# Softmax weights turned by VectorE and DMA instead of TensorE, in a two-layer hybrid trunk on one core

## The chip, the cores and the metric

The kernel runs on one core of one Trainium2 chip, as one launch. The metric is the device time of the whole program in microseconds, lower being better. The engines are TensorE (PE, with its weight loads shown as PEld), VectorE (DVE), ScalarE (ACT), GpSimd (POOL) and SyncE (SP, which only issues DMAs here). Each works through its own queue strictly in order and waits for the others through semaphores.

## The reference

The input is 256 tokens of width 2048, in float32. Layer one is a gated DeltaNet mixer, layer two a chunked softmax attention with 16 heads of width 128; each adds its output to its input. The part that matters is layer two (condensed):

```python
proj = rms_norm(h, norm_w[1]) @ w_in                  # 2048 -> 4 * 2048: q, k, v, z
q, k = rms_norm(q, q_norm_w), rms_norm(k, k_norm_w)   # per head
s = einsum('bchd,bmhd->bhcm', q_n, k_n) * scale + bias
p = softmax(where(valid, s, -inf))                    # each frame: its own and earlier chunks
o = einsum('bhcm,bmhd->bchd', p, v_n)
h = h + (o * silu(z)) @ w_out
```

With 256 tokens every earlier chunk lies in the band, so the attention is causal by chunks of 64. A head's weights are 128 queries by 128 keys for the first half of the tokens and 128 by 256 for the second: 384 columns on 128 partitions.

## The kernel before

Activations are kept with features on partitions and tokens along the row. All projections run as split float32: each weight chunk (512 KB, 128 rows of 1024 floats in SBUF) is loaded by SP into `wt` (4 buffers), rounded by ACT into `whi` (L206) and the rest taken by DVE into `wlo` (L207), 3 buffers each. PE then does the matmuls of L255 on them. Chunks are fetched three ahead (`LOOK`). A cast of a new chunk waits until PE has finished with the chunk three before it; a load waits until DVE has finished with the one four before it.

Layer two's q, k and v are projected by blocks of 512 columns, four heads each, with tokens on partitions: k and q of group 0, then of groups 1, 2 and 3, then v of groups 0 to 3. A block is 8 chunks of 12 matmuls. All other work of a group is put behind those matmuls in small steps (a queue of generators, `bgq`, stepped between matmuls), and the scheduler that builds the program sets the final order on each engine:

- `qk_norm`: the square (ACT, L1051) into a buffer named `cv`, the sum (DVE, L1054), the reciprocal root (POOL, L1056 and L1058), the product (DVE, L1063) into another `cv`, the transposes (PE, L1073). There are two `cv` buffers.
- `attend`: for each head the scores (PE, L1092 and L1093), bias and maximum (DVE, L1101), exponentials with their sums (ACT, L1105), the division (DVE, L1111 and L1113). Then `turned`: three 128 by 128 transposes (PE, L1119) into PSUM and a copy (ACT, L1120) to the place that `weights_of` gives: heads 0 to 9 in `kT`, heads 10 to 15 in `dl`.
- `values`, after each v block: for each head two matmuls (L1149 and L1150) of the values with the turned weights, then the gate (DVE, ACT).

A float32 matmul of L1092, L1093, L1149 or L1150 is two instructions in the trace; a transpose is one.

Of the kernel before, what the change touches and what calls it, by code (L numbers as in the profile page):

```python
# [7 lines left out]
F32 = mybir.dt.float32  # L8
# [6 lines left out]
P = 128  # L15
D = 2048
# [22 lines left out]
def tile_hybrid_trunk(  # L39
# [11 lines left out]
    nc = tc.nc  # L51
    act, dve, pool, pe = nc.scalar, nc.vector, nc.gpsimd, nc.tensor
# [9 lines left out]
    def ps_small():  # L62
        return pss.tile([P, 512], F32, name="pss", tag="pss")

    def wk(tag, bufs=None):

        return work.tile([P, 4, T], F32, name=tag, tag=tag, bufs=bufs)

    def slot(tag, kb, dt=F32):

        return big.tile([P, kb * 256], dt, name=tag, tag=tag)
# [15 lines left out]
    ps = ps_small()  # L87
# [4 lines left out]
    ident = const.tile([P, P], F32, name="ident")  # L92
# [222 lines left out]
    def block(kind, xb, rate=1, pre=None):  # L315
        ps = acc(kind)
        for _ in range(CPH if kind == "half" else CPB):
            chunk(kind, ps, xb, rate, pre)
        return ps
# [10 lines left out]
    def pair(xb, rate=1, pre=None):  # L330

        evs = []
        for _ in range(2):
            joined(block("half", xb, rate, pre), evs)
        return evs
# [72 lines left out]
    rows = ctx.enter_context(tc.tile_pool(name="rows", bufs=1, space=bass.MemoryType.DRAM))  # L408
# [379 lines left out]
    def gated_tiles():  # L788
        gmem["b"] = slot("g", 32, F32R).rearrange("p (h a t) -> p h a t", h=H, a=2)
        gmem["h"], gmem["l"] = (gmem["b"][:, :, a, :] for a in range(2))  # L790
# [132 lines left out]
    for gi in range(4):  # L923
        if gi == 0:
            bgq.append(x_stats())
        ps = pair(xb, 2) if gi else block("features", xb, pre=x_split)
# [12 lines left out]
    for gi in range(4):  # L939
        ps = pair(xb, 2)  # L940
# [6 lines left out]
    hmem = {}  # L947
# [36 lines left out]
    bmem = {}  # L984
# [33 lines left out]
    def zb_small(gi, evs):  # L1018
        z = bmem["z"][:, 4 * gi:4 * gi + 4, :]
        scaled(z, evs, scales["h"][1])  # L1020

        bias, hs = bmem["bias"], slice(4 * gi, 4 * gi + 4)
        dve.tensor_copy(out=bias[0:1, 4 * gi, 0:1], in_=z[0:1, 0, 0:1])
        nc.gpsimd.dma_start(out=bias[:, hs, :], in_=relb[:, hs, :])
        pool.memset(bias[0:64, hs, 192:256], NEG)
        yield 1
        act.activation(out=z, in_=z, func=AF.Silu)
        yield 1
# [14 lines left out]
    for j in (1, 2, 3):  # L1043
        bgq.append(zb_small(j, pair(xb)))

    def qk_norm(ps, scale, dst):

        ssn = tiny.tile([P, 2, 4], F32, name="ssn", tag="so")
        rn = tiny.tile([P, 2, 4], F32, name="rn", tag="ro")
        sq = wk("cv").rearrange("p h t -> p (h t)")  # L1050
        act.activation(out=sq, in_=ps.rearrange("p t d -> p (t d)"), func=AF.Square)  # L1051
        yield 1
        yield 1
        dve.reduce_sum(out=ssn, in_=sq.rearrange("p (t h d) -> p t h d", t=2, d=P), axis=AX.X)  # L1054
        for t in range(2):
            pool.tensor_scalar(out=ssn[:, t, :], in0=ssn[:, t, :], scalar1=1.0 / P, scalar2=bmem["uh"][:, t:t + 1],  # L1056
                               op0=ALU.mult, op1=ALU.add)
        pool.tensor_tensor(out=rn, in0=ssn, in1=nhalf[:, :8].rearrange("p (t h) -> p t h", t=2), op=ALU.pow)  # L1058
        yield 1
        yield 1  # L1060
        n = wk("cv").rearrange("p h t -> p (h t)").rearrange("p (t d) -> p t d", t=2)
        for t in range(2):
            dve.tensor_tensor(out=n[:, t, :].rearrange("p (h d) -> p h d", d=P),  # L1063
                              in0=ps[:, t, :].rearrange("p (h d) -> p h d", d=P),
                              in1=rn[:, t, :].unsqueeze(2).broadcast_to([P, 4, P]), op=ALU.mult)
        yield 1
        yield 1
        for p in range(2):
            pt = ps_small()
            for i in range(2):  # L1070
                c = (2 * p + i) * P
                for t in range(2):
                    pe.transpose(pt[:, i * T + t * P:i * T + (t + 1) * P], n[:, t, c:c + P], ident)  # L1073
            d = dst[:, 2 * p:2 * p + 2, :].rearrange("p h t -> p (h t)")
            if scale is None:
                act.copy(out=d, in_=pt)
            else:
                act.activation(out=d, in_=pt, func=AF.Copy, scale=scale)
            yield 1

    def attend(gi, qn, kn):
        if gi == 0:
            gated_tiles()
            gmem["done"] = 0
            bmem["w"] = slot("kT", 16)
        st = {}

        def scores(i):
            h = 4 * gi + i
            bias = bmem["bias"]  # L1090
            ps = ps_small()
            pe.matmul(ps[:, 0:128], lhsT=qn[:, i, 0:128], rhs=kn[:, i, 0:128], start=True, stop=True)  # L1092
            pe.matmul(ps[:, 128:384], lhsT=qn[:, i, 128:256], rhs=kn[:, i, :], start=True, stop=True)  # L1093
            if i == 0:
                st["s"] = wk("raw", 1).rearrange("p h t -> p (h t)")
            s = st["s"][:, 384 * (i % 2):384 * (i % 2 + 1)]
            mx = tiny.tile([P, 2], F32, name="mx", tag="mx")
            sums = tiny.tile([P, 2], F32, name="sums", tag="sums")
            parts = ((0, 128, bias[:, h, 128:256]), (128, 384, bias[:, h, :]))
            for t, (a, b, bi) in enumerate(parts):  # L1100
                dve.tensor_tensor_reduce(out=s[:, a:b], in0=ps[:, a:b], in1=bi, scale=1.0, scalar=-3e38,  # L1101
                                         op0=ALU.add, op1=ALU.max, accum_out=mx[:, t:t + 1])
            dve.tensor_scalar(out=mx, in0=mx, scalar1=-1.0, scalar2=None, op0=ALU.mult)
            for t, (a, b, _) in enumerate(parts):
                act.activation(out=s[:, a:b], in_=s[:, a:b], func=AF.Exp, bias=mx[:, t:t + 1],  # L1105
                               accum_out=sums[:, t:t + 1])
            st[i] = (s, sums)

        def weights(i):
            s, sums = st[i]  # L1110
            dve.reciprocal(out=sums, in_=sums)  # L1111
            for t, (a, b) in enumerate(((0, 128), (128, 384))):
                dve.tensor_scalar(out=s[:, a:b], in0=s[:, a:b], scalar1=sums[:, t:t + 1], scalar2=None, op0=ALU.mult)  # L1113

        def turned(i):
            s, _ = st[i]
            ps = ps_small()
            for a in (0, 128, 256):
                pe.transpose(ps[:, a:a + P], s[:, a:a + P], ident)  # L1119
            act.copy(out=weights_of(4 * gi + i), in_=ps[:, :384])  # L1120

        stages = (scores, weights, turned)
        for n in range(4 + len(stages) - 1):
            for k in reversed(range(len(stages))):
                if 0 <= n - k < 4:
                    stages[k](n - k)
            yield 1

    def weights_of(h):

        if h < 10:
            return bmem["w"][:, 384 * h:384 * h + 384]
        c = 2 * D + 384 * (h - 10)
        return hmem["m"][:, c:c + 384]

    def vb_small(gi, ps):
        c = (8192, 10240, 9216, 11264)[gi]
# [6 lines left out]
    def values(gi):  # L1144
        v = bmem["v"]
        for h in range(4 * gi, 4 * gi + 4):
            pT, vs = weights_of(h), slice(h % 4 * P, (h % 4 + 1) * P)
            ps = ps_small()
            pe.matmul(ps[:, 0:256], lhsT=v[:, 0, vs], rhs=pT[:, 0:256], start=True, stop=False)  # L1149
            pe.matmul(ps[:, 128:256], lhsT=v[:, 1, vs], rhs=pT[:, 256:384], start=False, stop=True)  # L1150
            gt = work.tile([P, T], F32, name="gt", tag="gt")
            dve.tensor_tensor(out=gt, in0=ps[:, :T], in1=bmem["z"][:, h, :], op=ALU.mult)
            act.copy(out=gmem["h"][:, h, :], in_=gt)
            dve.tensor_tensor(out=gmem["l"][:, h, :], in0=gt, in1=gmem["h"][:, h, :].bitcast(F32), op=ALU.subtract)
            gmem["done"] = h + 1
            yield 1

    for gi in range(4):
        c = 1024 * (gi % 2)
# [10 lines left out]
    for gi in range(4):  # L1170
        bgq.append(vb_small(gi, block("tokens", xb)))
        bgq.append(values(gi))
# [28 lines left out]
    ps = [ps_small().rearrange("p (a t) -> p a t", a=2) for _ in range(2)]  # L1201
# [6 lines left out]
    for s in range(2):  # L1208
# [3 lines left out]
        for j, kt in enumerate(ks):  # L1212
            stop = kt == KT - 1
# [7 lines left out]
        for j, kt in enumerate(ks):  # L1221
            pe.matmul(ps[s][:, 0, :], lhsT=lo[:, j, fs], rhs=gmem["b"][:, kt, 0, :], start=False,
                      stop=kt == KT - 1, skip_group_check=True)
# [46 lines left out]
```

## Time and profile before

| | us |
|---|---|
| median of 3 runs | 997.7 |
| lowest and highest | 997.11, 998.75 |
| the profiled execution | 998.12 |
| its span in the trace | 996.4 |
| PE busy | 990.2 |
| DVE busy | 685.7 |
| ACT busy | 537.3 |
| POOL busy | 71.2 |

The profiled execution's own time is 1.7 us above the span of its instructions. A row of a group gives line, engine, operation, output and inputs, shape and count, then busy time and the mean of one in ns, then the engine's idle time before them and what ended it. A row of a timeline starts with the start in us from the span's start and the duration of the merged instructions. A row of DMA issues ends with the KB of one and the median us from issue to landing. The k, q and v blocks of layer two lie between about 630 and 910 us; the 48 transposes of L1119 lie between 677.9 and 837 us.

### The profile page before, as it was taken

To read this page: it belongs to the slowest core of one execution; us is meant where nothing else is said; L and a number is where in the kernel's file an instruction comes from. 1 tells how busy PE (TensorE), PEld (TensorE's weight loads), DVE (VectorE), ACT (ScalarE), POOL (GpSimd) and SP (SyncE) were. 2 spreads that over 40 slices of the span, in tenths; PEclk is the share of its full clock that TensorE was granted. 3 is DMA by queue.
4 is the path that set the end of the run, shared out by engine and by line. 5 is a ranking of instruction groups with operands and counts; after the bars stand their busy time and mean duration, and the time that the engine had idled before them with its cause. 6 is when DMAs were issued, how large, how long until landed. Compare 5 with 4: busy or idle time off the path is not lost.

```text
span 996.4 us, 15340 instructions
## 1 busy us (share of the span) xinstructions
PE 990.2 (99%) x5915; PEld 862.7 (87%) x5915; DVE 685.7 (69%) x1114; ACT 537.3 (54%) x769; POOL 71.2 (7%) x97
## 2 busy tenths in 40 slices
PE   9999999999999999999999999999999999999998
PEld 7988888888888898899888888888888888888887
DVE  7788787997999768665776555556565656555554
ACT  8455887655447556445654444446454545444442
POOL 1002100122000001100000000110101010000000
PEclk9999999999999999999999999999999999999999
DMA  9668775545666543447666676665656555555672
GB/s 291 190 169 237 211 209 162 156 148 169 190 192 172 139 135 106 142 142 242 214 190 199 205 213 210 188 190 151 187 152 186 158 181 148 171 177 172 212 221 83
DMA packets 138953, 179.67 MB, mean 180 GB/s; under 512 B 8048, under 2 KB 98560, under 8 KB 138880
## 3 DMA queue, kind: packets, MB, share of 16 engines
q1 hardware_dynamic: 136832, 172.12, 58.0%
q0 software_dynamic: 1760, 6.31, 1.8%
q8 instruction: 46, 0.75, 0.3%
q10 hardware_dynamic: 288, 0.26, 0.1%
q14 instruction: 27, 0.22, 0.1%
HBM read 176.56 MB, written 2.11 MB: 179 GB/s over the span
## 4 chain that ended last, share of the span: by engine, by line
PE 97%; ACT 1%; DMA 1%; issue 1%; DVE 0%; SPq 0%
PE psp L255 86%; PE pss L601 2%; PE pss L255 1%; PE pss L838 1%; PE pss L1073 1%; PE pss L1093 1%; PE pss L1149 1%; DMA g<-in_xT_dram 1%; PE pss L1119 1%; ACT whi L206 1%; PE pss L737 0%; PE pss L824 0%; PE pss L845 0%; PE pss L861 0%; PE pss L860 0%
## 5 line engine op out<-in xcount | busy, mean ns | idle before, releaser
L207 DVE TENSOR_TENSOR wlo<-wt,whi 128x1024 fp32r<-128x1024 f32 (+2 forms) x324 | 390.9, 1210 | 248.2 <-ACT whi L206 246.7
L206 ACT CAST whi<-wt 128x1024 fp32r<-128x1024 f32 (+2 forms) x324 | 336.6, 1040 | 371.4 <-PE psp L255 331.1
L255 PE MATMUL psp<-whi,xb 128*128 128x512 f32 x1024 | 320.3, 392 | 0.0
L255 PE MATMUL psp<-xb,whi 128*128 128x512 f32 (+1 forms) x1088 | 258.3, 381 | 0.5 <-ACT whi L206 0.3
L255 PEld LDWEIGHTS psp<-xb,whi 128*128 128x128 f32 x1088 | 196.0, 190 | 34.7 <-ACT whi L206 0.8
L255 PEld LDWEIGHTS psp<-whi,xb 128*128 128x128 f32 x1024 | 192.1, 188 | 38.8
L255 PE MATMUL psp<-wlo,xb 128*128 128x512 f32 x512 | 200.9, 392 | 0.0
L255 PE MATMUL psp<-xb,wlo 128*128 128x256 f32 x1024 | 147.5, 285 | 0.7 <-DVE wlo L207 0.6
L255 PEld LDWEIGHTS psp<-xb,wlo 128*128 128x128 f32 x1024 | 137.0, 191 | 7.0 <-DVE wlo L207 1.8
L255 PE MATMUL psp<-g,whi 128*128 128x512 f32 (+1 forms) x608 | 131.6, 347 | 0.2 <-DVE ev L326 0.2
L255 PEld LDWEIGHTS psp<-g,whi 128*128 128x128 f32 x608 | 104.4, 190 | 13.0 <-DVE ev L326 0.6
L255 PEld LDWEIGHTS psp<-wlo,xb 128*128 128x128 f32 x512 | 96.2, 188 | 19.3
L255 PE MATMUL psp<-g,wlo 128*128 128x256 f32 x480 | 82.3, 283 | 0.0
L255 PEld LDWEIGHTS psp<-g,wlo 128*128 128x128 f32 x480 | 69.8, 191 | 1.8
L518 DVE SCALAR_TENSOR_TENSOR cv<-raw,sm,cv 128x255 f32<-128x255 f32 (+2 forms) x144 | 64.0, 480 | 5.2 <-ACT cv L516 4.9
L516 ACT ACTIVATE cv<-raw,sm 128x256 f32<-128x256 f32 x48 | 22.2, 501 | 10.4 <-DVE raw L341 10.4
L326 DVE TENSOR_TENSOR ev<-psp,ev 128x512 f32<-128x512 f32 x37 | 25.3, 683 | 0.1
L325 ACT COPY ev<-psp 128x512 f32<-128x512 f32 x37 | 21.4, 579 | 2.5 <-DVE raw L341 2.5
L1056 POOL TENSOR_SCALAR ssn<-ssn,uh 128x4 f32<-128x4 f32 x16 | 9.2, 592 | 171.6 <-DVE ssn L1054 171.6
L605 DVE TENSOR_TENSOR dl<-pss,dl 128x512 f32<-128x512 f32 (+1 forms) x32 | 16.5, 551 | 1.6 <-PE pss L601 1.6
L873 POOL TENSOR_TENSOR ro<-so,nhalf 128x8 f32<-128x8 f32 x4 | 8.4, 2104 | 122.4 <-DVE so L871 122.4
L1063 DVE TENSOR_TENSOR cv<-psp,rn 128x512 f32<-128x512 f32 x16 | 10.3, 684 | 9.2 <-POOL rn L1058 9.2
(246 smaller groups left out, 734.1 us busy)
## 6 DMA issues: line engine op xcount, KB each, us to landing
wt<-in_b_w_in_dram SPq DMA_DIRECT2D x128, 512.0 KB, 3.7
wt<-in_a_w_in_dram SPq DMA_DIRECT2D x125, 512.0 KB, 4.1
wt<-in_a_w_out_dram SPq DMA_DIRECT2D x32, 512.0 KB, 3.9
wt<-in_b_w_out_dram SPq DMA_DIRECT2D x32, 512.0 KB, 3.5
tt<-line POOLq DMA_DIRECT2D x4, 512.0 KB, 9.1
dl<-in_xT_dram POOLq DMA_DIRECT2D x4, 512.0 KB, 5.9
dl<-in_relb_dram POOLq DMA_DIRECT2D x4, 512.0 KB, 5.0
g<-in_xT_dram SPq DMA_DIRECT2D x7, 256.0 KB, 6.6
```

The costliest lines, as they stand in the source:

```text
L206: cast = act.copy(out=hi[:, js, cs], in_=wt[:, js, cs])
L207: rest = dve.tensor_tensor(out=lo[:, js, cs], in0=wt[:, js, cs], in1=hi[:, js, cs].bitcast(F32), op=ALU.subtract)
L255: state["mm"] = pe.matmul(*args, **kw).ins
L325: act.copy(out=ev, in_=ps[:, :, 1, :])
L326: dve.tensor_tensor(out=ev, in0=ps[:, :, 0, :], in1=ev, op=ALU.add)
L516: act.activation(out=cv[:, i, :], in_=raw[:, i, :], func=AF.Copy, scale=conv_w(i0 + i, 3))
L518: dve.scalar_tensor_tensor(out=cv[:, i, s:], in0=raw[:, i, :T - s], scalar=conv_w(i0 + i, 3 - s), in1=cv[:, i, s:], op0=ALU.mult, op1=ALU.add)
L601: pe.matmul(dst, lhsT=kq[:, a, i, c:c + P], rhs=rhs, start=(n == 0), stop=(n == 2))
L605: dve.tensor_tensor(out=dl[:, h, :, c], in0=src.rearrange("p (k c) -> p k c", k=2), in1=dec[:, h, c].unsqueeze(1).broadcast_to([P, 2, n]), ...
L838: pe.matmul(ps[:, i * P:(i + 1) * P], lhsT=tt[:, 2 * (h0 + i) + t, :], rhs=vb[:, i, t, :], start=True, stop=True)
L1063: dve.tensor_tensor(out=n[:, t, :].rearrange("p (h d) -> p h d", d=P), in0=ps[:, t, :].rearrange("p (h d) -> p h d", d=P), in1=rn[:, t, :] ...
L1073: pe.transpose(pt[:, i * T + t * P:i * T + (t + 1) * P], n[:, t, c:c + P], ident)
```

## The change

`turned` no longer uses PE and ACT. DVE's block transpose turns each 32 by 32 block of a head's 128 x 384 weights where it stands, and writes the blocks of two heads into one new `cv` buffer (768 floats a partition). After the second head of a pair, `regroup` sends that buffer to a DRAM tile (one DMA) and reads it back so that the blocks come to the partitions where they belong (four DMAs, each to 32 partitions, in runs of 192 floats). All 8 x 5 DMAs are issued by POOL. The weights of a pair now stand in a different order, so `values` reads its moving operand in runs of 32 floats.

```diff
+    def regroup(dst, u):
+        trips[0] += 1
+        m = rows.tile([P, 4, 32 * u.shape[1]], F32, name="trip%d" % trips[0])
+        nc.gpsimd.dma_start(out=m, in_=u.rearrange("p x c j -> p c (x j)"))
+        for c in range(4):
+            nc.gpsimd.dma_start(out=dst[32 * c:32 * c + 32].rearrange("i r x j -> i r (x j)"),
+                                in_=m[:, c, :].rearrange("(r i) y -> i r y", r=4))
...
         def turned(i):
-            s, _ = st[i]
-            ps = ps_small()
-            for a in (0, 128, 256):
-                pe.transpose(ps[:, a:a + P], s[:, a:a + P], ident)
-            act.copy(out=weights_of(4 * gi + i), in_=ps[:, :384])
+            if i % 2 == 0:
+                u = wk("cv").rearrange("p h t -> p (h t)")[:, :768]
+                st["u"] = u.rearrange("p (c x j) -> p x c j", c=4, j=32)
+            x = 3 * (i % 2)
+            dve.transpose(out=st["u"][:, x:x + 3], in_=st[i][0].rearrange("p (x c i) -> p x c i", c=4, i=32))
+            if i % 2:
+                regroup(weights_of((4 * gi + i) // 2), st["u"])
...
     def values(gi):
...
-            pT, vs = weights_of(h), slice(h % 4 * P, (h % 4 + 1) * P)
+            pT, vs = weights_of(h // 2), slice(h % 4 * P, (h % 4 + 1) * P)
+            x = 3 * (h % 2)
+            pT0, pT1 = pT.rearrange("p r x j -> p x r j")[:, x:x + 2], pT[:, :, x + 2, :]
             ps = ps_small()
-            pe.matmul(ps[:, 0:256], lhsT=v[:, 0, vs], rhs=pT[:, 0:256], start=True, stop=False)
-            pe.matmul(ps[:, 128:256], lhsT=v[:, 1, vs], rhs=pT[:, 256:384], start=False, stop=True)
+            pe.matmul(ps[:, 0:256].rearrange("p (x r j) -> p x r j", x=2, j=32), lhsT=v[:, 0, vs], rhs=pT0,
+                      start=True, stop=False)
+            pe.matmul(ps[:, 128:256].rearrange("p (r j) -> p r j", j=32), lhsT=v[:, 1, vs], rhs=pT1,
+                      start=False, stop=True)
```

Lines after the new function are 11 higher in the changed kernel up to `turned`: L1051 becomes L1062, L1056 and L1058 become L1067 and L1069, L1063 becomes L1074, L1092 and L1093 become L1103 and L1104, L1105 becomes L1116. The DVE turn is L1131, the DMAs are L1052 and L1054, the values' matmuls L1162 and L1164.

The scheduler also orders the work of a group anew. On PE before, after group 0's q block: two heads' scores, then later transposes of one head between the scores of the next. (`pss` is a PSUM bank, `raw` the weights, `dl` q, k and bias; the numbers tell buffers apart.)

```order
L1092 MATMUL pss_6600<-dl_4897 128x128 [waits Activation_49]
L1093 MATMUL pss_6600<-dl_4897 128x256
L1092 MATMUL pss_6620<-dl_4897 128x128 [waits PE_49]
L1093 MATMUL pss_6620<-dl_4897 128x256
...
L1119 MATMUL pss_6642<-ident_94,raw_6603 128x128 [waits DVE_49,PE_49]
L1092 MATMUL pss_6650<-dl_4897 128x128 [waits PE_49]
L1119 MATMUL pss_6642<-ident_94,raw_6603 128x128 [waits DVE_49]
```

The same place on PE after: the scores of all four heads stand together.

```order
L1103 MATMUL pss_6600<-dl_4897 128x128 [waits Activation_49]
L1104 MATMUL pss_6600<-dl_4897 128x256
L1103 MATMUL pss_6620<-dl_4897 128x128 [waits PE_49]
L1104 MATMUL pss_6620<-dl_4897 128x256
L1103 MATMUL pss_6647<-dl_4897 128x128 [waits Activation_49]
L1104 MATMUL pss_6647<-dl_4897 128x256
```

The transposes are gone from PE's queue, and heads 2 and 3 moved up by some 33 projection matmuls. The transposes of the next group's keys, which followed the last L1119, now stand 24 projection matmuls later.

On POOL after, in the same group (`trip` is the DRAM tile, `ssn` and `rn` belong to the next group's `qk_norm`; before, POOL had only the rows of `ssn` and `rn` there):

```order
L1052 DMA trip1_6664<-cv_6642 128x768 [waits DMASW5_49,DVE_49]
L1054 DMA kT_6599<-trip1_6664 32x4x192 [waits DMAHW1_49,DMASW6_49,DMASW5_49]
...
L1052 DMA trip2_6707<-cv_6695 128x768 [waits DVE_49]
L1067 TENSOR_SCALAR ssn_6744<-ssn_6744,uh_5457 128x4 [waits DVE_49,Pool_49]
L1069 TENSOR_TENSOR rn_6745<-ssn_6744,nhalf_103 128x8 [waits Pool_49]
L1054 DMA kT_6599<-trip2_6707 32x4x192 [waits DMASW2_49]
```

The first pair's read back waits for its write to land, and the second pair's write and then the next group's reciprocal root stand behind it.

On ACT after, at the square of the next group's keys (before, this row had no wait and stood before the exponentials of heads 2 and 3):

```order
L206 CAST whi_6714<-wt_6713 128x1024 [waits DMAHW3_49,PE_49]
L1116 ACTIVATE raw_6603,sums_6677<-raw_6603,mx_6676 128x128 [waits DVE_49,Activation_49]
L1116 ACTIVATE raw_6603,sums_6677<-raw_6603,mx_6676 128x256
L206 CAST whi_6733<-wt_6732 128x1024 [waits DMAHW4_49,PE_49]
L1062 ACTIVATE cv_6746<-psp_6490 128x1024 [waits DMASW5_49]
L206 CAST whi_6755<-wt_6754 128x1024 [waits DMAHW5_49,PE_49,Activation_49]
```

The square now waits for the first pair's write (DMASW5), with the cast of a weight chunk behind it.

More of the change, by code (lines that the diff above doesn't have):

```diff
@@ L1044, in tile_hybrid_trunk @@
         bgq.append(zb_small(j, pair(xb)))
+    trips = [0]
+    def regroup(dst, u):
[5 more added lines that the diff above has]
+                                in_=m[:, c, :].rearrange("(r i) y -> i r y", r=4))
     def qk_norm(ps, scale, dst):
@@ L1127, in attend, with weights_of @@
             yield 1
[L1129 to L1134, printed above, removed]
+    def weights_of(pr):
+        w = bmem["w"][:, 768 * pr:768 * pr + 768] if pr < 5 else hmem["m"][:, 2 * D + 768 * (pr - 5):2 * D + 768 * (pr - 4)]
+        return w.rearrange("p (r x j) -> p r x j", r=4, j=32)
     def vb_small(gi, ps):
```

## The prediction

> **What bounds the kernel now.** I read the page's busy shares and its chain first, then the busy time in windows over layer two's q/k/v stage, where the change lies, then the timeline of TensorE there.
>
> ```profile
> span 996.4 us, 15340 instructions
> PE 990.2 (99%) x5915; PEld 862.7 (87%) x5915; DVE 685.7 (69%) x1114; ACT 537.3 (54%) x769; POOL 71.2 (7%) x97
> PE 97%; ACT 1%; DMA 1%; issue 1%; DVE 0%; SPq 0%
> ...
> 675.00:720.00 45.00, 45.00 (x219) 37.80 (x218) 26.74 (x44) 23.37 (x35) 5.32 (x6) 1.00 0.58 175
> ```
>
> TensorE (PE) is busy in 99% of the span and carries 97% of the chain. The window row gives, after the window's length, PE, weight loads, VectorE (DVE), ScalarE (ACT) and GpSimd (POOL): PE is busy for all 45.00 us, DVE for 26.74, ACT for 23.37; the granted clock is 1.00, the DMA engines are 0.58 busy. But a pipelined PE can look busy while it waits, so its cadence is needed too.
>
> ```profile
> 674.53 0.39 PE L255 MATMUL psp<-wlo,xb 128*128 128x512 f32 x1
> 674.75 0.62 PE L255 MATMUL psp<-whi,xb 128*128 128x512 f32 x2
> 675.21 0.39 PE L255 MATMUL psp<-wlo,xb 128*128 128x512 f32 x1
> ...
> 689.46 0.82 PE L1119 MATMUL pss<-ident,raw 128*128 128x128 f32 x6
> 690.11 1.04 PE L1073 MATMUL pss<-ident,cv 128*128 128x128 f32 x8
> ```
>
> Three projection matmuls take 675.21 - 674.53 = 0.68 us, 0.227 each, and a weight chunk of 12 takes 2.72 us. Six of the transposes that the change removes (L1119) start at 689.46, and what follows them starts at 690.11: 0.65 / 6 = 0.109 us each, back to back. Their inputs were ready and nothing beside them is hidden: in this stage each 0.109 us is the program's time.
>
> **The transposes that go.** The groups between 640 and 900 us:
>
> ```profile
> L206 ACT CAST whi<-wt 128x1024 fp32r<-128x1024 f32 x84 | 88.4, 1053 | 113.2 <-PE psp L255 105.2 <-DVE cv L1063 6.7 <-ACT raw L1105 0.9
> L1119 PE MATMUL pss<-ident,raw 128*128 128x128 f32 x48 | 8.2, 273 | 0.0
> L1149 PE MATMUL pss<-kT,dl 128*128 128x256 f32 x20 | 5.5, 379 | 0.0
> L1120 ACT COPY kT<-pss 128x384 f32<-128x384 f32 x10 | 4.6, 477 | 1.9 <-PE pss L1119 1.9
> ```
>
> 48 x 0.109 = 5.2 us leave PE. That group's 8.2 us and its mean of 273 ns count each matmul from issue to a modelled end, so they overlap their neighbours; I take the cadence. [...]
>
> The copies out of PSUM (16 x 477 ns = 7.6 us) leave ACT. That is worth nothing by itself: the cast's idle time of 113.2 us was ended by PE for 105.2 of it, so ACT has time over.
>
> **The block turns that come.** A neighbour is the turn in layer one:
>
> ```profile
> L549 DVE STREAM_TRANSPOSE dl<-cv 128x512 f32<-128x512 f32 x8 | 5.4, 696 | 0.0
> ...
> L672 DVE STREAM_TRANSPOSE g<-g 128x1024 f32<-128x1024 f32 x1 | 2.2, 2153 | 0.0
> ```
>
> For 384 elements that is between 696 x 384/512 = 0.52 us and, by the row that writes across its blocks, 2153 x 384/1024 = 0.81 us. The new turn writes runs of 32 in blocks set apart, between the two; I take 0.65. 16 x 0.65 = 10.4 us on DVE, hidden in the time that it idles (18 us of the 45 above). What could end this cover is the order, taken up below.
>
> **The values' matmuls.** L1149 and L1150 stay, 32 instructions each, but their moving operand is now read in runs of 32 floats.
>
> ```profile
> L255 PE MATMUL psp<-xb,wlo 128*128 128x256 f32 x1024 | 147.5, 285 | 0.7 <-DVE wlo L207 0.6
> L601 PE MATMUL pss<-tt 128*128 128x256 f32 x24 | 4.8, 280 | 0.0
> ```
>
> L601's 256-column form reads two runs of 128 with a gap, and takes 280 ns where the unbroken 256 columns of L255 take 285. I take nothing for the runs. The bound on the other side is a doubling of 64 matmuls at their cadence (0.22 us for 256 columns, 0.11 for 128): 32 x 0.33 = 10.6 us. Below nothing I see no reason: the columns are as many.
>
> **The trips through DRAM.** Eight pairs of heads, each one write and four reads of 384 KB in all either way, all issued by POOL.
>
> ```profile
> tt<-line POOLq DMA_DIRECT2D x4, 512.0 KB, 9.1
> dl<-in_relb_dram POOLq DMA_DIRECT2D x4, 512.0 KB, 5.0
> out_dram<-ev SPq DMA_DIRECT2D x7, 256.0 KB, 4.6
> line<-kT POOLq DMA_DIRECT2D x1, 16.0 KB, 2.8
> ...
> 607.73 0.53 POOL L1024 DMA_DIRECT2D dl<-in_relb_dram  x1 [16.59 <-DVE dl L1023]
> ```
>
> A write of 384 KB, from issue to landing, lies between 2.8 us (16 KB to DRAM) and 9.1 (512 KB, four queued at once). By the rows nearest in size (256 KB to DRAM 4.6, 512 KB from DRAM 5.0) I take 5; an issue takes POOL 0.53 us. The values read the weights a block or more later, so the read back has tens of us. SP's queue, which issues the weight loads, gets none of the new DMAs. Added traffic: 8 x 0.79 MB = 6.3 MB over some 175 us, 36 GB/s on the 175 of the window, or a DMA share of about 0.70. The weight loads have room:
>
> ```profile
> wt<-in_b_w_in_dram SPq DMA_DIRECT2D x128, 512.0 KB, 3.7
> ...
> 668.11 1.22 DVE L207 TENSOR_TENSOR wlo<-wt,whi 128x1024 fp32r<-128x1024 f32 x1 [2.40 <-ACT whi L206]
> ...
> 671.05 1.05 ACT L206 CAST whi<-wt 128x1024 fp32r<-128x1024 f32 x1 [2.98 <-PE psp L255]
> ...
> 681.26 1.05 ACT L206 CAST whi<-wt 128x1024 fp32r<-128x1024 f32 x1 [1.11 <-PE psp L255]
> ```
>
> The subtraction that ends at 669.33 frees the buffer whose next content is cast at 681.26, four chunks on; 3.7 us of those 11.9 are the load. So 8.2 us are spare there, and contention costs nothing.
>
> **The new waits.** This is what can give the gain back. The turned pair sits in a "cv" buffer, and the square of the next group's keys (L1051; L1062 after) needs that buffer: ACT now waits at the square for the pair's write to land, and behind it in ACT's queue stands the cast of the next chunk. Three groups are followed by such a square.
>
> ```profile
> 669.32 0.38 PE L1092 MATMUL pss<-dl 128*128 128x128 f32 x2
> ...
> 670.43 0.81 PE L255 MATMUL psp<-whi,xb 128*128 128x512 f32 x2
> ...
> 670.17 0.29 DVE L1101 CUSTOM_DVE_ANT_0 raw<-pss,dl 128x128 f32<-128x128 f32 x1 [0.84 <-PE pss L1093]
> ...
> 671.57 0.17 DVE L1103 TENSOR_SCALAR mx<-mx 128x2 f32<-128x2 f32 x1
> ...
> 674.43 0.17 DVE L1111 RECIPROCAL sums<-sums 128x2 f32<-128x2 f32 x1 [1.07 <-ACT raw L1105]
> 674.63 0.55 DVE L1113 TENSOR_SCALAR raw<-raw,sums 128x128 f32<-128x128 f32 x2
> ...
> 677.54 1.01 ACT L1051 ACTIVATE cv<-psp 128x1024 f32<-128x1024 f32 x1
> 678.82 1.21 DVE L1054 TENSOR_REDUCE ssn<-cv 128x8 f32<-128x1024 f32 x1
> 680.13 0.51 POOL L1056 TENSOR_SCALAR ssn<-ssn,uh 128x4 f32<-128x4 f32 x2 [20.80 <-DVE ssn L1054]
> 680.72 1.64 POOL L1058 TENSOR_TENSOR rn<-ssn,nhalf 128x8 f32<-128x8 f32 x1
> ```
>
> I lay the new order on these durations. Two heads' scores hold PE from 669.32 to about 670.6, 1.31 us. Four now go at once, so PE frees weight buffers 1.3 us later than the 671.05 above: at 672.4, then each 2.72 us to 683.2 and 686.0. After head 1's scores (671.7) DVE does: the wait for head 0's exponentials (0.5), its weights (0.72) and turn (0.65), a subtraction (1.23), head 2's scores (0.95), head 1's weights (0.72), a subtraction (1.23), head 1's turn (0.65). That ends at 678.4, and the write is issued. ACT comes to the square at 682.1, behind a cast freed at 680.5. With a landing after L = 5 us the square starts at 683.4, a wait of 1.3; then 1.01, the reduction 1.21 and the next subtraction 1.23 end at 686.9. PE needs that one at 688.9, a chunk after 686.0 and one matmul. Spare: 2.0, so the wait is paid from L = 7.0 on.
>
> A second way goes through POOL: landing, four issues (2.1), the next pair's write (0.5), then L1056 and L1058 (2.2), which now stand behind those DMAs; the normalisation that DVE stops at (2 x 0.65) and a subtraction 1.23 end at 678.4 + L + 7.3, and PE needs that one at 694.4: spare until L = 8.7, or about 6 if issues take twice as long. I take 6.5 as the point from which a late landing costs, 3 x (L - 6.5). At L = 5: nothing.
>
> **Sum.** 48 x 0.109 off PE, nothing for the rest: -5.2 us. The profiled execution took 998.12 us (span 996.4 and 1.7 around it), so 992.9; it stands 0.4 above the median of 997.7, from which it would be 992.5. I forecast 992.7.
>
> **Rivals.** First, the write lands late. For it: L's upper row is 9.1 us, the write meets weight loads that hold the DMA engines at 0.58, and POOL may be slow to issue. Against: single transfers of 512 KB landed in 5.0. It costs 3 x (L - 6.5): at 7.5 us 995.7, at 9.1 us 7.8 and so 1000.5; from L = 8.2 the gain is gone. [...]
>
> Second, the strided read. If runs of 32 floats halve the rate, it costs 10.6 and gains 5.2: 1003.1, slower. It decides from half of that doubling. For it: no row has runs of 32. Against: L601.
>
> Third, the trips crowd out the weight loads. Casts would have to wait for wt by more than those 8 us of spare; some 3 to 6 us in all, 996 to 999. Fourth, a transpose is worth its 273 ns: 13.1 off, 985.0; the cadence is against it.
>
> **Chances.** The forecast 0.70, with 991.8 to 994.0 for its own range (turns and landing within the spare, a run's spread); late landing 0.16; strided read 0.07; crowding 0.04; the larger gain 0.03. About 0.2% (2 us) is what a measurement can tell from no change: faster means under 995.7, slower over 999.7. Faster: 0.70 + 0.03 + half of the late landings 0.08 = 0.81. Slower: 0.07 and the latest landings 0.02 = 0.09. Same: the rest, 0.10. The range goes from 991.8 to 997.5, which takes in the forecast and most of the late landings.
>
> **What would show it.** In the changed profile L1119 and L1120 are gone; the DVE turn shows 16 times at 0.5 to 0.8 us; PE stays busy for all of 675 to 720 with 0.227 a matmul; the square (L1062) shows a DMA wait of 0 to 2 us, three times; L1162 and L1164 stay near 379 and 275 ns. Wrong would be: gaps on PE ended by ACT's cast or DVE's subtraction about 686 to 695 us (a late landing), L1162 well above 379 ns (the strided read), or a cast that waits for wt (crowding).

## The result, and the profile after

The changed kernel takes 991.47 us (median of 4 runs, 990.94 to 991.68) against 997.4 for the kernel before beside it (4 runs, 997.06 to 998.75). The ratio is 0.9941, with a 95% interval of 0.9927 to 0.9954: faster by 0.6%, some 5.9 us. The forecast was 992.7 with a low end of 991.8, so the sign and the mechanism held and the time lies 0.33 us under the range. The profiled execution took 991.34 us.

First the page of the changed kernel (span, busy times, chain).

```profile
span 989.6 us, 15303 instructions
PE 983.0 (99%) x5867; PEld 856.8 (87%) x5867; DVE 693.3 (70%) x1130; ACT 530.4 (54%) x753; POOL 97.2 (10%) x137
PE 97%; ACT 1%; DMA 1%; issue 1%; DVE 0%; SPq 0%
```

And its window over 675 to 720 us, with the columns as before.

```profile
675.00:720.00 45.00, 45.00 (x213) 37.67 (x212) 28.59 (x49) 22.58 (x35) 11.25 (x16) 1.00 0.74 221
```

TensorE still fills the window and the chain, so nothing new became the bound. In the window DVE went from 26.74 to 28.59, POOL, which the row of before has at 5.32, to 11.25, the DMA share from 0.58 to 0.74. Of PE's 5915 matmuls 48 are gone, and the span is 6.8 us shorter.

The groups between 640 and 900 us:

```profile
L206 ACT CAST whi<-wt 128x1024 fp32r<-128x1024 f32 x86 | 90.4, 1051 | 106.8 <-PE psp L255 99.2 <-issue 5.9 <-DVE cv L1074 1.7
...
L1131 DVE STREAM_TRANSPOSE cv<-raw 128x384 f32<-128x384 f32 x16 | 9.2, 574 | 0.2
...
L1062 ACT ACTIVATE cv<-psp 128x1024 f32<-128x1024 f32 x7 | 7.2, 1024 | 2.4 <-DMA trip<-cv 2.4
...
L1162 PE MATMUL pss<-kT,dl 128*128 128x256 f32 x20 | 5.1, 378 | 0.0
```

A turn takes 574 ns; the squares wait 2.4 us in all for the trips; the values' matmul with its strided operand takes 378 ns, as unbroken ones did. No cast waits for `wt`: of the 106.8 us of idle time before the casts PE ended 99.2, as before, and for another 5.9, five casts, the profile names no cause, but each of these starts 0.08 us after the end of a chunk on PE. The DMA issues (KB of one, median us to landing):

```profile
wt<-in_b_w_in_dram SPq DMA_DIRECT2D x128, 512.0 KB, 3.8
...
trip<-cv POOLq DMA_DIRECT2D x8, 384.0 KB, 4.7
...
kT<-trip POOLq DMA_DIRECT2D x20, 96.0 KB, 5.4
```

The weight loads land in 3.8 us where they took 3.7. And the place of the new wait, in group 0, on POOL, ACT, DVE and PE:

```profile
677.06 0.64 POOL L1052 DMA_DIRECT2D trip<-cv  x1 [18.92 <-DVE sums L1122]
681.51 2.22 POOL L1054 DMA_DIRECT2D kT<-trip  x4 [3.82 <-DMA trip<-cv]
683.72 0.56 POOL L1052 DMA_DIRECT2D trip<-cv  x1
684.32 0.72 POOL L1067 TENSOR_SCALAR ssn<-ssn,uh 128x4 f32<-128x4 f32 x2
...
681.25 1.03 ACT L1062 ACTIVATE cv<-psp 128x1024 f32<-128x1024 f32 x1 [0.83 <-DMA trip<-cv]
682.17 1.04 ACT L206 CAST whi<-wt 128x1024 fp32r<-128x1024 f32 x1
...
683.45 1.22 DVE L207 TENSOR_TENSOR wlo<-wt,whi 128x1024 fp32r<-128x1024 f32 x1
...
687.54 0.39 PE L255 MATMUL psp<-wlo,xb 128*128 128x512 f32 x1
```

The write is issued at 677.06 and lands at 681.25, after 4.2 us; the square waits 0.83 for it. The subtraction behind it ends at 684.67, and PE came to its result at 687.54: 2.9 us were still spare.

Where did the time go? Two lines bracket every one of the transposes: the first scores and the last values' matmuls. Their rows give duration (least, median, most, in ns) and the start of the first and the last one, of the kernel before and then of the changed one:

```profile
L1092 PE MATMUL pss<-dl x32: 270/274/276, 669.3 to 827.6; 128*128 128x128 f32 x32
L1150 PE MATMUL pss<-dl x12: 272/276/276, 883.4 to 907.6; 128*128 128x128 f32 x12
```

```profile
L1103 PE MATMUL pss<-dl x32: 271/273/276, 668.1 to 814.3; 128*128 128x128 f32 x32
L1164 PE MATMUL pss<-dl x12: 272/275/276, 876.7 to 900.9; 128*128 128x128 f32 x12
```

From 669.3 to 907.6 are 238.3 us; from 668.1 to 900.9 are 232.8. So 5.5 of the 6.8 us went here. The other 1.2 were there before the first score, where nothing was changed (669.3 against 668.1): that part belongs to the run.

To divide a span more finely I count the 4784 projection matmuls of L255, which are the same in every kernel here. *Start* is the time to the end of number 768, counted from 0; *middle*, from there to number 3360 (group 0's q block is done); *stage*, to number 4128 (the other k and q blocks, and two v blocks: the change's work lies here); *tail*, the rest of the span.

| profiled run | span | start | middle | stage | tail |
|---|---|---|---|---|---|
| before | 996.41 | 138.29 | 521.67 | 201.91 | 134.54 |
| before, again | 995.64 | 137.55 | 521.66 | 201.92 | 134.51 |
| after | 989.63 | 137.11 | 521.66 | 196.34 | 134.52 |
| after, again | 990.14 | 137.62 | 521.66 | 196.34 | 134.52 |
| transposes twice | 1000.78 | 137.24 | 521.66 | 207.35 | 134.53 |
| 48 alone | 996.61 | 137.38 | 521.65 | 203.06 | 134.51 |
| no trip | 990.65 | 138.14 | 521.67 | 196.34 | 134.50 |
| late by one | 990.38 | 137.79 | 521.65 | 196.41 | 134.53 |
| late, small runs | 989.59 | 136.91 | 521.67 | 196.50 | 134.51 |
| late by six | 1010.96 | 138.35 | 521.66 | 216.44 | 134.51 |
| late by POOL | 992.63 | 137.03 | 521.67 | 199.42 | 134.52 |
| keys too | 987.08 | 138.21 | 520.76 | 193.59 | 134.52 |
| keys and queries too | 1001.13 | 137.41 | 520.75 | 208.44 | 134.52 |

The stage repeats to 0.01 us and the change took 5.57 off it. All that differs between two traces of one kernel is the start: by 0.74 us before and 0.51 after. Over all thirteen traces it lies within 1.4 us.

### The profile page after: what moved, and what is told of

Read it like the earlier page. It is cut to its first block, busy times and chain, and to the rows that moved or that the text cites. A ratio compares the mean times of both kernels' runs of the same rounds, so it can differ in the third digit from the quotient of the medians.

```text
span 989.6 us, 15303 instructions
## 1 busy us (share of the span) xinstructions
PE 983.0 (99%) x5867; PEld 856.8 (87%) x5867; DVE 693.3 (70%) x1130; ACT 530.4 (54%) x753; POOL 97.2 (10%) x137
## 4 chain that ended last, share of the span: by engine, by line
PE 97%; ACT 1%; DMA 1%; issue 1%; DVE 0%; SPq 0%
PE psp L255 86%; PE pss L601 2%; PE pss L255 1%; PE pss L838 1%; PE pss L1084 1%; PE pss L1104 1%; PE pss L1162 1%; DMA g<-in_xT_dram 1%; ACT whi L206 1%; PE pss L737 0%; PE pss L824 0%; PE pss L845 0%; PE pss L861 0%; PE pss L859 0%; PE pss L860 0%
## 5 line engine op out<-in xcount | busy, mean ns | idle before, releaser
L255 PE MATMUL psp<-whi,xb 128*128 128x512 f32 x1024 | 320.5, 392 | 0.0
L255 PE MATMUL psp<-xb,whi 128*128 128x512 f32 (+1 forms) x1088 | 257.3, 380 | 1.0 <-ACT whi L206 0.8
L255 PEld LDWEIGHTS psp<-whi,xb 128*128 128x128 f32 x1024 | 192.0, 188 | 38.9
L255 PEld LDWEIGHTS psp<-xb,whi 128*128 128x128 f32 x1088 | 195.2, 189 | 34.9 <-ACT whi L206 1.0
L255 PE MATMUL psp<-wlo,xb 128*128 128x512 f32 x512 | 200.8, 392 | 0.0
L255 PE MATMUL psp<-xb,wlo 128*128 128x256 f32 x1024 | 146.9, 284 | 0.7 <-DVE wlo L207 0.5
L255 PEld LDWEIGHTS psp<-xb,wlo 128*128 128x128 f32 x1024 | 136.5, 191 | 6.7 <-DVE wlo L207 1.5
L255 PE MATMUL psp<-g,whi 128*128 128x512 f32 (+1 forms) x608 | 131.6, 347 | 0.2 <-DVE ev L326 0.2
L255 PEld LDWEIGHTS psp<-g,whi 128*128 128x128 f32 x608 | 104.4, 190 | 13.0 <-DVE ev L326 0.6
L255 PEld LDWEIGHTS psp<-wlo,xb 128*128 128x128 f32 x512 | 96.2, 188 | 19.2
L255 PE MATMUL psp<-g,wlo 128*128 128x256 f32 x480 | 82.3, 283 | 0.0
L255 PEld LDWEIGHTS psp<-g,wlo 128*128 128x128 f32 x480 | 69.8, 192 | 1.8
L1116 ACT ACTIVATE raw<-raw,mx 128x128 f32<-128x128 f32 (+1 forms) x32 | 14.3, 447 | 12.5 <-DVE mx L1114 12.5
L1074 DVE TENSOR_TENSOR cv<-psp,rn 128x512 f32<-128x512 f32 x16 | 10.3, 685 | 9.2 <-POOL rn L1069 9.2
```

The source lines that it names most:

```text
L255: state["mm"] = pe.matmul(*args, **kw).ins
```

## The experiments

**The kernel before, and the changed one, a second time** (no edit).

> The kernel before, unchanged, as a second trace of it. In the two traces so far the changed kernel was already 1.2 us ahead at the 768th projection matmul of the program (137.1 against 138.3 us), long before the changed stage. Theory: that lead is the spread of the program's start from run to run; this trace then reaches that matmul somewhere between 136.8 and 138.5 us, and times spread over 1 us or more around 997.4. Rival: the lead belongs to the changed program; then this trace repeats 138.3 within 0.1 us.

Measured: 997.36 us (11 runs, 996.64 to 997.7), ratio 1.0001 (0.9992 to 1.001), stage 201.92. Its start was 137.55 and not 138.29 again: the lead of the changed kernel belongs to the run and not to the program.

> The changed kernel, unchanged, a second time. Theory: the time between the projection matmuls 3360 and 4128 is fixed by the program, and the runs differ only in when the program's first projections get going. So that stretch comes out at 196.34 us again (within 0.05), and what differs from the first profile of this kernel lies ahead of matmul 768 (137.1 us there; 136.9 to 138.3 in the kernels run so far). Its median should lie 5.3 to 6.2 us under that of the kernel before, and, against a run of this kernel that starts as late as the first profile of before (138.29), the profiled execution would take about 992.6. Rival: the stage itself varies from run to run (by 0.3 us, what the forecast was short by); then the stretch comes out away from 196.34 by some tenths.

Measured: 991.67 us (5 runs, 991.15 to 991.87) against 997.26, ratio 0.9942 (0.9929 to 0.9956); stage 196.34. Its start was 137.62, later by 0.51 than in the first profile, and its span longer by 0.51. In the traces the spread of runs is the start's, and the first profile of before, on which the forecast was built, had nearly the latest start of all.

**Each transpose twice.** In the kernel before:

```diff
-            for a in (0, 128, 256):
+            for a in (0, 0, 128, 128, 256, 256):
                 pe.transpose(ps[:, a:a + P], s[:, a:a + P], ident)
```

> The kernel before with each of the 48 transposes of L1119 done twice into the same place. Theory: TensorE is the bound throughout the stage and a transpose costs its cadence of 0.109 us: 48 x 0.109 = 5.2 more, 5.2 to 5.6 with the new order's interruptions, so 1002.6 to 1003.0 us. Rival: a transpose costs its 273 ns: 13.1 more, 1010.5 us. Rival: some of it hides: under 4 more.

The transposes, in the same columns as above:

```profile
L1119 PE MATMUL pss<-ident,raw x96: 270/273/274, 677.1 to 840.0; 128*128 128x128 f32 x96
```

Measured: 1002.63 us (1002.35 to 1002.82) against 997.17, ratio 1.0056 (1.0042 to 1.007). The stage is 5.44 longer: 48 more transposes, each of which the row still puts at 273 ns, cost 0.113 each. In this full stream the price of a transpose was its cadence, not its duration; the rival of 273 ns is out.

**48 transposes, scattered.** The changed kernel, with a transpose of the identity in front of a weight chunk, 48 times over the same blocks:

```diff
+        if "w" in bmem and alone[0] < 48:
+            alone[0] += 1
+            with behind():
+                pt = ps_small()
+                pe.transpose(pt[:, 0:P], ident, ident)
```

> The changed kernel with 48 extra transposes of the identity on TensorE, spread over the stage in some 40 places of their own between projection matmuls, read by nobody. It asks where the 0.34 us came from that the stage gained beyond 48 x 0.109 us. Theory: each interruption of the stream of projection matmuls makes the next few of them slower, some 0.03 us in all; then the stage between projection matmuls 3360 and 4128 grows from 196.34 by 5.2 + 40 x 0.03 = 6.4 to 202.8 us. Rival: an interruption costs nothing but its own cadence: 201.6 us.

The added transposes, ns least, median and most, first and last start:

```profile
L297 PE MATMUL pss<-ident x48: 270/272/273, 669.7 to 813.7; 128*128 128x128 f32 x48
```

Measured: one run of 998.32 us, stage 203.06, which is 6.72 above the changed kernel's: 0.140 each, where 48 that stood next to each other cost 0.113 or less. Not every one stands alone: some come in pairs or beside other small matmuls, and the stream of projection matmuls is broken at 49 places where the changed kernel breaks it at 19. Laid out by the ends of the matmuls, the other matmuls take 27.08 us as in the kernel before (27.10; 21.82 in the changed one), and the projection's 768 take 175.98 instead of 174.52. So 1.46 us went to the projection matmuls around 30 more breaks of their stream: in all kernels in which PE does not stop the first seven to ten after a break take up to 12 ns more than their 0.227 us, 0.01 to 0.05 us a break where that many follow. The same split of the change itself: 27.10 to 21.82 is 5.28 for the transposes, and 174.81 to 174.52 another 0.29 around the breaks: 21 became 19, and four of these stand a single matmul behind another one. (Far from a break a projection matmul takes 0.2268 us in both kernels.) That is the 5.57, where the forecast has 5.2. Why a break costs this no run here takes apart.

**No trip.** The turn writes straight to the weights' place, with no DMA; the values then use weights whose blocks stand on the wrong partitions.

```diff
-            dve.transpose(out=st["u"][:, x:x + 3], in_=st[i][0].rearrange("p (x c i) -> p x c i", c=4, i=32))
-            if i % 2:
-                regroup(weights_of((4 * gi + i) // 2), st["u"])
+            dst = weights_of((4 * gi + i) // 2).rearrange("p r x j -> p x r j")
+            dve.transpose(out=dst[:, x:x + 3], in_=st[i][0].rearrange("p (x c i) -> p x c i", c=4, i=32))
```

> The changed kernel with the block turn written straight to the place of the weights and all 40 DMAs left out; the regrouping is left out, so the values use weights in a wrong order. Theory: the trips are hidden, their only trace is the square's wait of 0.8 us three times, which uses spare time: 991.5 us within 0.3, and between projection matmuls 3360 and 4128 the same TensorE time within 0.1 us. Rival: the waits or the traffic cost TensorE: up to 2.4 us faster, about 989.1.

Measured: 992.08 us (991.2 to 992.37), ratio 0.9949 (0.9937 to 0.9962), stage 196.34, equal to the changed kernel's to the hundredth. 40 DMAs, 6.3 MB, the wait of the squares: hidden altogether. (The order is not quite the same here: the transposes of the next group's keys stand 15 projection matmuls earlier.) The median is not lower than the changed kernel's, and need not be: the profiled start of this one is 138.14.

**How late may a trip land?** Four variants of the changed kernel, each run once. One extra write of 384 KB to a scratch tile in DRAM ahead of each group's first write; the same in runs of 32 floats; six extra writes; or six multiplications by 1.0 on GpSimd instead. The first and the last two, condensed, with comments added:

```diff
         trips[0] += 1
+        for n in range(1 if trips[0] % 2 else 0):      # late by one; 6 for late by six
+            extra = rows.tile([P, 4, 32 * u.shape[1]], F32, name="extra%d_%d" % (trips[0], n))
+            nc.gpsimd.dma_start(out=extra, in_=u.rearrange("p x c j -> p c (x j)"))
...
+        for n in range(6 if trips[0] % 2 else 0):      # late by POOL
+            nc.gpsimd.tensor_scalar(out=flat, in0=flat, scalar1=1.0, scalar2=None, op0=ALU.mult)
```

> The changed kernel with one more 384 KB write of the same buffer to DRAM ahead of each group's first write, so that this one lands some 1.5 to 2 us later (4.2 us before). The order on the engines stays but for the keys' transposes, 9 projection matmuls later. Theory: the square's wait grows from 0.8 to 2.4 to 3 us, three times, and the spare of about 3 us beyond a landing of 4.2 still covers it: stage 196.34 within 0.1 us, 991.5 us. Rival, by the point of 6.5 us that the prediction took, or if the spare is smaller: gaps on TensorE, up to 3 us in all.

POOL and ACT in group 0, where the extra write stands and where the square waits:

```profile
677.74 0.64 POOL L1053 DMA_DIRECT2D extra<-cv  x1 [18.92 <-DVE sums L1125]
...
683.15 1.03 ACT L1065 ACTIVATE cv<-psp 128x1024 f32<-128x1024 f32 x1 [2.06 <-DMA trip<-cv]
```

Measured: 992.45 us, stage 196.41. The trip lands 5.4 us after the point at which it was issued before (677.74 to 683.15, against 4.2), the square waits 2.06 us, and 0.07 us of the stage is all that is lost; 0.06 of that lies in the projection matmuls around three more breaks (22 against 19). The spare takes the lateness, as the prediction had it up to 6.5.

> As the last, but the extra write goes out in runs of 128 bytes (3072 of them), so that the group's first write lands much later, 8 to 15 us after its issue; the scheduler put the square two casts later and the keys' transposes 23 projection matmuls later. Theory: once the landing passes what the order leaves spare (some 10 us here), TensorE waits: three gaps of the landing minus 10 us, 0 to 15 us in all on the stage's 196.34. Rival: TensorE never sees the write, however late: 196.34 within 0.1.

Measured: 991.33 us, stage 196.50. The trips landed in 4.2 to 7.3 us (median 6.5), not the 8 to 15 that I expected, an estimate that no run stood behind, and the squares waited only 0.6 in all. The reason is not spare: in this program the order on ACT has the square of the next keys behind two more casts. The order is worked out from modelled times when the program is built, and it moved, so the theory was not put to the test. The 0.16 us lost are again in the projection matmuls (174.68 against 174.52), around 25 breaks for 19.

> The changed kernel with six extra writes of 384 KB to scratch ahead of the first write of each group. One extra write moved the landing of the first write by 1.2 us, so here it lands some 4.2 + 6 x 1.2 = 11.5 us after the turn. Theory: the order of the instructions is worked out when the program is built, from modelled times that see the late landing; it puts the square of the keys behind four more casts, where nothing waits for it for long, and TensorE loses next to nothing: the stretch between the projection matmuls 3360 and 4128 stays between 196.3 and 197.3 us. Rival (the prediction's price of a late landing in a fixed order): from 6.5 us on each of three squares costs what the landing is late, 3 x (11.5 - 6.5) = 15 us, a stretch of about 211 us; by the spare that the trace of the changed kernel shows (7.3 us) 3 x 4.2 = 12.6, about 209.

Measured: 1012.67 us, stage 216.44, 20.1 above the changed kernel. My theory falls, and the rival's mechanism is not what the trace shows either. First the waits of PE between 600 and 900 us and of ACT between 640 and 880 (us in total, times, longest):

```profile
PE pss L1087 <- DVE cv L1077: 14.1, 4, 5.3
...
ACT whi L206 <- DMA wt<-in_b_w_in_dram: 24.3, 10, 4.0
```

Then the timeline of ACT, DVE and PE in group 0:

```profile
692.75 1.05 ACT L206 CAST whi<-wt 128x1024 fp32r<-128x1024 f32 x1 [2.93 <-DMA wt<-in_b_w_in_dram]
693.70 1.02 ACT L1065 ACTIVATE cv<-psp 128x1024 f32<-128x1024 f32 x1
...
701.98 1.23 DVE L207 TENSOR_TENSOR wlo<-wt,whi 128x1024 fp32r<-128x1024 f32 x1 [2.74 <-ACT whi L206]
703.12 1.28 DVE L1077 TENSOR_TENSOR cv<-psp,rn 128x512 f32<-128x512 f32 x2
...
703.86 0.44 PE L1087 MATMUL pss<-ident,cv 128*128 128x128 f32 x2 [4.26 <-DVE cv L1077]
```

No square waits for a trip. The casts wait 24.3 us for weight loads that land late beside the extra writes: between 676 and 700 us a load takes 8.2 us (median), against 4.9 in the changed kernel. That is the third rival, crowding, at seven times the traffic of a group's first write. The product (L1077) that the keys' transposes read has to wait as well: the square stands behind one such cast, the subtraction that DVE does just before the product behind another, and the transposes of the keys, at a fixed place in PE's order, come before their input is ready.

Then a second price, by the windows (PE, PEld, DVE, ACT, POOL, granted clock, DMA share, GB/s):

```profile
704.00:707.50 3.50, 3.34 (x12) 2.72 (x12) 1.53 (x2) 1.33 (x2) 1.78 (x3) 0.57 0.64 194
708.50:712.00 3.50, 3.50 (x17) 2.88 (x16) 1.20 (x2) 1.05 (x1) 0.00 (x0) 1.00 0.00 0
```

After PE's stop of 4.26 us the granted clock is 0.57 over the next 3.5 us and projection matmuls end 0.43 us apart instead of 0.227; then it is 1.00 again. The half clock lasts 3.41 us, once in each of three groups (the run's mean clock of 0.995 over its span of 1011.0 us makes some 10 us of it in all); by these figures that costs 3 x 1.7 = 5.1 us, an estimate, and with the stops' 14.1 makes 19.2 of the 20.1. What sets the clock down the trace does not show.

> The changed kernel with six multiplications by 1.0 in place on GpSimd ahead of the first write of each group: the write is made late by work on POOL, with no byte more to move. By the nearest rows (128x512 in 785 ns, 128x1024 in 957) six take about 5 us, and with the issues that the order puts between them the first write lands some 11 to 12 us after the turn, about as late as with the six extra writes, where the stretch between the projection matmuls 3360 and 4128 was 216.4 us. Theory: there the traffic did it (casts waited 24 us for weight loads that landed late behind the extra writes), and a late landing that the order was laid out for costs little: here the stretch is 196.3 to 198 us. Rival: the late square did it, whatever made it late; then TensorE stops here too at the keys' transposes in each of the three groups, some 4 to 6 us each, and the stretch is 208 us or more.

The instructions of the added line (ns least, median, most; first and last start), then PE's waits:

```profile
L1053 POOL TENSOR_SCALAR cv<-cv x24: 2121/2144/3189, 676.9 to 838.8; 128x768 f32<-128x768 f32 x24
```

```profile
PE pss L1087 <- DVE cv L1077: 1.7, 6, 0.6
```

Measured: 994.34 us, stage 199.42, 3.1 above the changed kernel: above what I gave for my theory (198), far from the rival's 208. An operation took 2.12 us or more, not the 0.8 I took from nearest rows, and the order put the second pair's write ahead of the first's, which was issued only at 700.22; the squares waited 4.5 us in all, and the small matmuls of the stage, the keys' transposes with their waits among them, took 2.97 us more (24.79 against 21.82), some 1 us in each of three groups. So lateness without traffic cost 3 us where lateness with traffic cost 20. Since the order was another one each time, this does not measure the price of a late landing in the order of the changed kernel; that it begins at 6.5 us stays an estimate.

**The keys' transposes as well.** The same exchange for the 32 transposes of the keys: two DVE turns and a trip for each group; the norm's weight goes to the queries' copy.

```diff
+        if turn:
+            trips[0] += 1
+            u = dst.rearrange("p (c h t j) -> p t h c j", c=4, h=4, t=2)
+            for t in range(2):
+                dve.transpose(out=u[:, t], in_=n[:, t, :].rearrange("p (h c i) -> p h c i", h=4, c=4))
...
+            nc.gpsimd.dma_start(out=m, in_=dst.rearrange("p (c y) -> p c y", c=4))
+            for c in range(4):
+                nc.gpsimd.dma_start(out=dst[32 * c:32 * c + 32].rearrange("i (r y) -> i r y", r=4),
+                                    in_=m[:, c, :].rearrange("(r i) y -> i r y", r=4))
```

> The changed kernel with the keys' 32 transposes (L1084) also replaced by block turns and a trip through DRAM (512 KB each way for each group; the norm weight moves to the queries' copy). Theory: the keys have a whole block of time before their scores, so the trip hides: 32 x 0.109 = 3.5 less plus 4 interruptions of about 0.03 us: 987.8 us. Rival: the scores wait for the keys, or GpSimd's queue holds back the queries' norm: gaps on TensorE, 990 to 995 us.

The turns that came and the transposes that stayed, in the groups between 640 and 900 us:

```profile
L1083 DVE STREAM_TRANSPOSE dl<-cv 128x512 f32<-128x512 f32 x7 | 4.6, 684 | 0.0
L1097 PE MATMUL pss<-ident,cv 128*128 128x128 f32 x32 | 4.1, 273 | 0.0
```

Measured: 988.8 us (4 runs, 988.62 to 989.29) against 997.17, ratio 0.9918 (0.9905 to 0.9932): faster than both kernels, and 1.0 above the 987.8 that I expected; the profiled start (138.21) is 1.1 later than that of the changed kernel. Stage and middle together are 3.65 shorter than the changed kernel's (group 0's transposes stood just ahead of the stage): 32 x 0.114. Only the queries' 32 transposes are left, in L1097. The trips' waits (squares 4.3 us in all) are still hidden: PE shows no wait between 600 and 900 us.

**The queries' transposes as well.** On top of that, the same for the queries, which come back into another buffer and are scaled into place by ACT.

```diff
+            to = dst if scale is None else wk("raw", 1).rearrange("p h t -> p (h t)")
...
+            if scale is not None:
+                act.activation(out=dst.rearrange("p (y r j) -> p y r j", r=4, j=32),
+                               in_=to.rearrange("p (r y j) -> p y r j", r=4, j=32), func=AF.Copy, scale=scale)
```

> The kernel with the keys' transposes replaced, and the queries' 32 transposes too (trip through DRAM into the scores' buffer, then scaled into place by ScalarE). Theory of a gain: another 32 x 0.109 + 4 x 0.03 = 3.6 us less on TensorE than with the keys alone, 988.8 - 3.6 = 985.2 us, if the trip of the queries (about 12 us from turn to scale) only moves the scores later. Rival: the scores now stand 38 to 60 projection matmuls later, and squares wait for buffers held longer: gaps, 986 to 992 us.

The waits of PE and ACT between 640 and 880 us, then a window:

```profile
PE psp L255 <- DVE cv L1074: 7.6, 3, 3.8
PE pss L1121 <- ACT dl L1093: 5.0, 4, 1.8
...
ACT dl L1093 <- DMA raw<-trip: 19.4, 4, 6.0
ACT cv L1062 <- DMA trip<-cv: 12.6, 6, 4.5
```

```profile
703.00:706.00 3.00, 3.00 (x8) 2.33 (x8) 2.58 (x3) 0.92 (x2) 2.75 (x7) 0.51 1.00 247
```

Measured: 1001.63 us (6 runs, 999.42 to 1004.43) against 997.49, ratio 1.0041 (1.0029 to 1.0054): slower than before and than the 992 of my rival. Here the cover is gone: the scores need the queries soon after their block, so ACT waits 19.4 us for them at the scaling copy (L1093), and PE stops for 5.0 us at the scores. The squares wait 12.6, and PE stops for another 7.6 us because the normalisation (L1074), which waits for the reciprocal root on POOL, has not yet freed a PSUM buffer. Two of its stops are followed by half clock (0.51 over 703 to 706 us). Against the version with the keys alone the stage is 14.9 longer. This is a late landing as the prediction feared it, at steps that have no slack.

## Why the prediction missed, point by point

**What bounds the kernel.** Right: PE, before and after, and the cadence of 0.109, not 273 ns, was close to the price of a transpose (5.28 / 48 = 0.110).

**The step that failed is the sum**: the way of the gain was right, and its terms were mis-sized. It reads "48 x 0.109 off PE, nothing for the rest: -5.2 us", set against 998.12 and 997.7, and the range "991.8 to 994.0" laid around it for "a run's spread". Forecast less result is 992.7 - 991.47 = 1.23 us, and it divides so:

- 0.37 is the term's size: the stage lost 5.57, not 5.2. The transposes gave 5.28 and fewer and closer breaks of the projection's stream 0.29, a term that the prediction's "nothing for the rest" left out without a reason.
- About 0.5 is the base. The forecast amounts to 997.9 less 5.2, but 998.12 was a run with the latest start but one of the thirteen in the table (138.29), and the median of 997.7 came from three runs; with a fourth it is 997.4, and the sets measured since have 997.17, 997.36, 997.49 and 997.26.
- The rest, 0.36, is not accounted for by a trace; it is within the start's spread of 1.4 us, and the second set of the changed kernel, 991.67, has 0.2 less of it.

With the right base and the right term the forecast would have been 997.4 - 5.57 = 991.8, the low end itself. The range left 0.9 us below the forecast for everything, less than the start's spread, while 4.8 us above it were kept for the late landing.

**ACT's copies, worth nothing.** Nothing contradicts it: they left, and the cast still waited for PE (99.2 of its 106.8 us).

**The block turn, 0.65 us within 0.52 to 0.81.** 0.574: right within the range. It was hidden: PE has no wait for it, and the transposes and the breaks account for the whole change of the stage.

**The strided operand, nothing against a bound of 10.6.** Right: 378 ns for the 256 columns, 275 for the 128, both as before. The keys' variant reads the scores' operand in such runs as well, again at 273 and 381.

**The trips.** L was taken as 5: the first write of a group landed in 3.9 to 4.2, the second in 5.2 to 6.3 (median of all eight 4.7). An issue took 0.56 to 0.64, against 0.53; four read-back issues 2.22, against 2.1. No write of the change took the 7.5 or the 9.1 us at which the late-landing rival is priced.

**The new wait, 1.3 us within 0 to 2, price from 6.5.** 0.74 to 0.83 us, three times, and nothing paid. The order laid out there held: with the 1.18 us added by which this run started earlier than the profile of before, the write is issued at 678.2 and PE needs the chunk at 688.7, where the prediction has 678.4 and 688.9; only the landing came sooner than the 5 us taken. With a landing at 5.4 next to nothing was paid either. When the queries were turned too, it was not the first way (square, cast, subtraction) that broke: PE's waits for a subtraction are 0.4 us there. It was the second, through POOL to the normalisation, with 7.6.

**The crowding rival.** Absent in the change, and real at a heavier load: six extra writes made the casts wait 24.3 us for their loads.

## What to carry to other kernels

Where TensorE was the bound and its stream full, a transpose of 273 ns taken out of it or put into it was worth its cadence and a little for the break it made, 0.11 to 0.14 us. A slow route over VectorE and DRAM was free here (a stage of 196.34 us with the trips and without), where the values read the weights tens of microseconds later; the same route for an operand that is needed at once lost more than everything it had won (1001.63 us against 997.49 for the kernel before). Before a gain of half a per cent is forecast, take the base from several runs and find which part of the span varies; the spread of the start was four times the error of the term. When an experiment adds work to a scheduled program, look at the order again: the plan itself moves, and the result may be that of another program.

## What the runs showed of the hardware that was not expected

- The parts of the program that an edit leaves alone repeat to 0.02 to 0.04 us (middle 521.65 to 521.67, tail 134.50 to 134.54); only the first 138 us vary, by 1.4 us, and most of that is there after some 20 us (0.81 of the 1.18 us between the first traces of before and after). Why is not shown.
- A break in a stream of projection matmuls cost some 0.01 to 0.05 us beside the instruction that makes it, spread over the seven to ten matmuls behind it (1.46 us for 30 more breaks, 0.06 for three more).
- A stop of TensorE of 2.31 us (ahead of the window at 703 us in the last experiment) was followed by half clock (0.51 over 703 to 706 us); the stops of up to 1.8 us in the same run were not.
- A multiplication of 128 x 768 on GpSimd took 2.1 to 3.2 us, while a fill of 128 x 1024 took 0.96.
